# Latent projections ahead of the context's feed-forward network, which runs beside the window attention, with the modulations one stage earlier

## The chip, the cores and the metric

The kernel runs on one core of a Trainium2 chip. A core has a matrix engine (TensorE, PE, whose weight loads are listed as PEld), a vector engine (VectorE, DVE), a scalar engine (ScalarE, ACT), a general engine (GpSimd, POOL) and a queue engine (SyncE, SP), which here issues every transfer between the device's main memory and the on-chip buffers. The metric is the device time of one execution in microseconds (us); lower is better.

## The reference, cut to what matters

A token stream x (512 tokens of 1024) passes two hybrid layers; then it and a context stream xc (256 tokens) pass two more blocks. The change concerns the first of those, the even block:

```python
for l in range(DEPTH):
    sh1, sc1, g1, sh2, sc2, g2 = split(s_c @ ada_w[l] + ada_b[l], 6)      # and csh1 ... cg2 from s_cc
    h  = rms_norm_2(x,  norm_g[l, 0]) * (1 + sc1)  + sh1
    hc = rms_norm_2(xc, norm_g[l, 0]) * (1 + csc1) + csh1
    y, yc = mixer_even(h, hc, ...)
    x = x + g1 * rms_norm_2(y, norm_g[l, 1])
    h = rms_norm_2(x, norm_g[l, 2]) * (1 + sc2) + sh2
    x = x + g2 * rms_norm_2(swiglu(h, ffn_w_in[l], ffn_w_out[l]), norm_g[l, 3])
    if l < DEPTH - 1:                                                      # the context, even block only
        xc = xc + cg1 * rms_norm_2(yc, norm_g[l, 1])
        hc = rms_norm_2(xc, norm_g[l, 2]) * (1 + csc2) + csh2
        xc = xc + cg2 * rms_norm_2(swiglu(hc, ffn_w_in[l], ffn_w_out[l]), norm_g[l, 3])

def mixer_even(h, hc):
    qa, ka, va, cq, ckv, kpe = split_cols(h @ w_in, EVEN_SIZES)            # window q, k, v; latents of q and kv; rotary key
    qb  = rms_norm_2(cq,  q_norm)  @ w_uq                                  # 8 heads of 64 + 32 rotary
    kvb = rms_norm_2(ckv, kv_norm) @ w_ukv                                 # 8 heads of 64 key + 64 value
    oa = windowed_sink_attention(qa, ka, va, ka_c, va_c, sink)             # local window and the context
    ob = softmax attention of qb over the keys of context and tokens
    return concatenate([oa, ob]) @ w_out
```

## The kernel before

**Products.** Activations lie with channels on the partitions, 8 tiles of 128 (KD = 8) by the tokens. Every product in single precision is taken as three products of halves: `split` makes hi and lo of an activation, `weights` loads 128 x 1024 of a weight (512 KB, tile wr, three buffers), lets ACT cast it to wh and POOL, or for every third one DVE, form wl (two buffers each). `dense` then does 24 matmuls for 128 output channels: wh with hi and lo for each of 8 input tiles, and wl with hi. `fm(i)` in `even_project` is such a dense with columns of ev_w_in: 0 to 3 window queries, 4 window key, 5 window value, 6 the latent of keys and values, 7 and 8 that of queries, 9 the rotary key.

**Memory.** The operand h of the token stream lies in hh and hl (2 x 16 KB a partition). Smaller tiles come from pool rp (nine buffers). Results that attention needs in another layout go by `put` (line 816) to scratch in main memory and come back by `get` (line 819): eka and eva (window key, value), eqm (window queries), ekn, ekp, evb (latent attention's key, rotary key, value), eqnm and eqpm (its queries). An rp tile is free again once its write has landed. All puts, gets and loads go through SP in one order.

**Order.** Each engine runs its instructions in the order of the program. `weave` runs several streams (Python generators) by turns in proportion to their rates; a third number is an offset in priority. `background` holds the modulations (`mods`: a chunk loads 2 tiles mr of ada_w, makes products with the two condition vectors and spreads them), and `tick` moves them on by a rate while a weave runs; `drain` finishes them. Twelve chunks of the groups (4, 3, 5) concern this block's second half.

**Stages around the change**, all in the function that quotes `even_project` (lines 1810 to 1860): `ctxa`, the second layer's output projection beside the context's own attention; `ctxo`, the residual and norm that give h (`boundary`) beside the context's output projection; `evp`, first `win()` (window projections fm 0 to 5) beside the context's residual, then in `win` the window attention `even_window` (two groups of four query heads, four blocks each) beside `lat()`. That `lat()` is in order: fm 6 and its norm; four products with ev_w_ukv for the keys, whose eight tiles are put to ekn; four products for the values (evb); fm 9 and the rotary key; fm 7, 8 and their norm; the products with ev_w_uq (eqnm, eqpm). After that come `lat`, the latent attention `even_latent` beside `context()` (norm, feed-forward network of the context (FFN), second norm, in memory of pool cf), the output projection, and the boundary before the main FFN, beside what is left of `context()`. In that weave the context has rate 48 to the attention's 9.6, and it stops when the attention ends.

## Time and profile before

| | us |
|---|---|
| three runs | 2822.88, 2830.22, 2830.51 |
| their median | 2830.22 |
| profiled execution | 2819.89 |
| its span in the trace | 2818.1 |
| PE busy | 2455.0 (87%) |
| DVE, ACT, POOL busy | 1258.7, 1188.2, 1079.4 |
| mean granted clock of PE | 0.918 |

The profile comes from one more execution. Stages are cut at instructions found in the trace: the first matmul with ev_w_in, the first window score, the first latent score, the first and last matmul of the output projection, and the first matmul of the main FFN.

### The profile page before, as it was taken

Reading aid. Unit: us, or ns where it says so; the run is one execution under the profiler, and the core shown is the slowest. Engines: PE = TensorE matmul, PEld = TensorE weight load, DVE = VectorE, ACT = ScalarE, POOL = GpSimd, SP = SyncE. Lnnn points to the kernel's source line nnn. Section 1 sums busy time; section 2 is a strip of 40 time slices with the busy share of each in tenths; the row PEclk is TensorE's granted clock in tenths of the full one; section 3 lists DMA queues with packets and bytes.
Section 4 is the critical chain, followed back from the end, with each engine's and each line's share of the span. In section 5 each row is a group of like instructions: output and inputs, shape, how many; then the busy total and the mean of one; then the engine's idle time right before and its main releaser. Section 6 shows DMA issues by size and latency. Waiting matters only on the chain. (4 is left out here: it accounts for less than half of the span.)

```text
span 2818.1 us, 35394 instructions
## 1 busy us (share of the span) xinstructions
PE 2455.0 (87%) x13052; PEld 1994.9 (71%) x13052; DVE 1258.7 (45%) x2065; ACT 1188.2 (42%) x2227; POOL 1079.4 (38%) x754
## 2 busy tenths in 40 slices
PE   6988896778888886769999899999888989799997
PEld 4765666666666665648998777777776777688886
DVE  3655357235646644445442631212645767421212
ACT  3534365333547534445554522222434646332222
POOL 2435235344533551213455732322542222443334
PEclk9988998888979987879999999999988989899998
DMA  7364644344344652335553545454444253333332
GB/s 244 121 205 156 207 165 154 107 140 162 104 124 139 213 182 100 116 112 143 174 159 135 186 135 172 149 169 133 148 140 158 90 153 113 113 100 97 94 97 75
DMA packets 170816, 400.56 MB, mean 142 GB/s; under 512 B 19378, under 2 KB 60820, under 8 KB 167316
## 3 DMA queue, kind: packets, MB, share of 16 engines
q1 hardware_dynamic: 170644, 398.31, 43.7%
q8 instruction: 103, 1.69, 0.2%
q14 instruction: 69, 0.57, 0.1%
HBM read 339.85 MB, written 58.39 MB: 141 GB/s over the span
## 5 line engine op out<-in xcount | busy, mean ns | idle before, releaser
L398 POOL TENSOR_TENSOR wl<-wr,wh 128x1024 fp32r<-128x1024 f32 (+3 forms) x245 | 538.2, 2198 | 899.5 <-ACT wh L422 451.5
L422 ACT CAST wh<-wr 128x1024 fp32r<-128x1024 f32 (+3 forms) x367 | 353.8, 964 | 706.5 <-PE d L389 279.5
L389 PE MATMUL d<-hh,wh 128*128 128x512 f32 x960 | 398.4, 415 | 19.7 <-ACT hh L556 7.8
L389 PE MATMUL d<-hl,wh 128*128 128x512 f32 x960 | 394.0, 410 | 1.9 <-DVE hl L557 0.9
L389 PE MATMUL d<-hh,wl 128*128 128x512 f32 x960 | 263.5, 403 | 0.0
L400 DVE SCALAR_TENSOR_TENSOR wl<-wr,wh 128x1024 fp32r<-128x1024 f32 (+3 forms) x122 | 152.1, 1246 | 227.8 <-PE d L389 91.9
L389 PEld LDWEIGHTS d<-hh,wh 128*128 128x128 f32 x960 | 190.6, 199 | 62.2 <-ACT hh L556 8.4
L389 PEld LDWEIGHTS d<-hl,wh 128*128 128x128 f32 x960 | 189.7, 198 | 42.5 <-issue 2.5
L389 PEld LDWEIGHTS d<-hh,wl 128*128 128x128 f32 x960 | 185.0, 195 | 39.6 <-issue 1.6
L400 DVE SCALAR_TENSOR_TENSOR pg<-b,pg 128x512 fp32r<-128x512 f32 (+1 forms) x208 | 137.2, 665 | 68.7 <-ACT pg L404 67.2
L389 PE MATMUL b<-hh,wh 128*128 128x512 f32 x416 | 164.2, 395 | 0.0
L389 PE MATMUL b<-hl,wh 128*128 128x512 f32 x416 | 163.2, 392 | 0.0
L934 POOL TENSOR_TENSOR oy<-pg,pg 64x256 f32<-64x256 f32 (+1 forms) x72 | 57.7, 802 | 262.3 <-DVE pg L932 91.3
L404 ACT CAST pg<-b 128x512 fp32r<-128x512 f32 (+1 forms) x208 | 117.1, 570 | 80.2 <-PE b L909 68.2
L882 DVE TENSOR_REDUCE sm<-s 128x1 f32<-128x768 f32 (+3 forms) x144 | 120.7, 846 | 26.6 <-PE s L389 25.9
L389 PE MATMUL d<-hc,wh 128*128 128x256 f32 x656 | 105.4, 311 | 23.7 <-DVE rp L400 11.8
L950 DVE SCALAR_TENSOR_TENSOR rp<-rp,d 128x512 f32<-128x512 f32 (+1 forms) x77 | 46.7, 607 | 165.5 <-ACT rp L949 165.4
L1745 DVE SCALAR_TENSOR_TENSOR rp<-rp,b 128x512 f32<-128x512 f32 (+1 forms) x64 | 38.1, 595 | 175.3 <-PE b L389 174.8
L389 PE MATMUL d<-hid,wh 128*128 128x512 f32 (+1 forms) x528 | 114.7, 361 | 1.5 <-POOL hid L398 1.5
L389 PEld LDWEIGHTS d<-hc,wh 128*128 128x128 f32 x656 | 94.9, 211 | 28.3 <-ACT wh L422 12.2
L389 PE MATMUL b<-hid,wh 128*128 128x512 f32 (+1 forms) x528 | 110.8, 361 | 0.0
L389 PE MATMUL b<-hh,wl 128*128 128x512 f32 x416 | 103.8, 389 | 0.0
(416 smaller groups left out, 5143.2 us busy)
## 6 DMA issues: line engine op xcount, KB each, us to landing
wr<-in_ffn_w_in SPq DMA_DIRECT2D x132, 512.0 KB
mr<-in_ada_w SPq DMA_DIRECT2D x96, 512.0 KB
wr<-in_ffn_w_out SPq DMA_DIRECT2D x48, 512.0 KB
x<-x SPq DMA_DIRECT2D x20, 1024.0 KB
wr<-in_w_in SPq DMA_DIRECT2D x38, 512.0 KB
mr<-in_w_mod SPq DMA_DIRECT2D x32, 512.0 KB
wr<-in_ev_w_in SPq DMA_DIRECT2D x20, 512.0 KB
wr<-in_ffn_w_out SPq DMA_DIRECT2D x24, 384.0 KB
```

Source lines behind the costliest of these rows:

```text
L389: self.nc.tensor.matmul(out, lhsT, rhs, start=start, stop=stop)
L398: self.nc.gpsimd.tensor_sub(out, src, hi)
L400: self.nc.vector.scalar_tensor_tensor(out, src, scale, hi, op0=ALU.mult, op1=ALU.subtract)
L404: self.nc.scalar.copy(hi, src)
L422: nc.scalar.copy(hi[:, :n], raw[:, :n])
L882: nc.vector.reduce_max(c, s, axis=AX.X, negate=True)
L934: nc.gpsimd.tensor_tensor(d, sel(t), sel(rs), op=ALU.mult)
L950: nc.vector.scalar_tensor_tensor(t, t, 1.0, ps, op0=ALU.add, op1=ALU.mult)
L1745: nc.vector.scalar_tensor_tensor(g, g, 0.5, pu, op0=ALU.mult, op1=ALU.mult)
```

## The change

- `even_project` is rearranged for the token stream: after fm 6 come fm 7 and 8 (`queries()`, tiles latq) and fm 9 (`rotary_key()`), and only then ukv and uq. The context's own order stays.
- The first three steps of `lat()` now run ahead of the window attention (`first(lt, 3)`), so that h is read for the last time before it.
- `context()` starts beside the window attention, with rate 22 to 8 (attention) and 4 (`lat`). Its operand lies in the memory of hl, its hidden units in that of hh. Pool cf goes. In the latent stage its rate is 36 instead of 48.
- The output projection reads its operand from a new pool `oh` (two tiles of 16 KB) in place of hh and hl.
- Modulations (4, 3, 5) run at rate 0.55 instead of 0.3 and are drained before `evp` rather than behind the window stage.
- The window attention has four query buffers instead of five.

```diff
--- before.py
+++ after.py
@@ -537,12 +537,12 @@
             except StopIteration as e:
                 return e.value
 
-    def prenorm_steps(self, x, T, gain, shift, pool=None, al=None):
+    def prenorm_steps(self, x, T, gain, shift, pool=None, al=None, into=None):
 
         nc = self.nc
         n = x.shape[1]
         r = self.rstd(self.square_sums([x[:, k, :] for k in range(n)], T, al), T, al=al)
-        h = self.new_h(T, pool)
+        h = into or self.new_h(T, pool)
         for k in range(n):
             self.norm_tile(h, x, k, T, r, gain, shift, al)
             yield
@@ -1417,7 +1417,7 @@
             self.split_ps(src, d[:, :, 0, :], d[:, :, 1, :])
             self.put(self.eva[:, c0 // 128 + t], d.rearrange("p h a d -> p h (a d)"))
 
-    def latent(self, fs, T, gains, pool):
+    def latent(self, fs, T, gains, pool, name="lat"):
 
         nc = self.nc
         xs = []
@@ -1429,7 +1429,7 @@
         out = []
         for i, (x, g) in enumerate(zip(xs, gains)):
             nc.vector.scalar_tensor_tensor(x, x, g, r, op0=ALU.mult, op1=ALU.mult)
-            hl = [self.tl(pool, [128, T], F32R, f"lat{i}{p}", 1) for p in range(2)]
+            hl = [self.tl(pool, [128, T], F32R, f"{name}{i}{p}", 1) for p in range(2)]
             self.split(x, *hl)
             out.append(hl)
         return out
@@ -1453,28 +1453,11 @@
             self.vtrans(fm(5), T, c0)
             yield
 
-        def latent():
-
-            (ck,) = self.latent([partial(fm, 6)], T, [self.mla_gain[:, 2:3]], pool)
-            hi, lo = self.weights(I["ev_w_ukv"], 1024)
-            for i in range(4):
-                w = slice(i * 128, i * 128 + 128)
-                ps = self.three(self.bank([128, T], "d"), [(hi[:, w], lo[:, w])], [ck])
-                parts = self.rp([128, T], F32R), self.rp([128, T])
-                self.split_ps(ps, *parts)
-                for hl, p in enumerate(parts):
-                    self.put(self.ekn[hl, :, 2 * i:2 * i + 2, c0:c0 + T].rearrange("r h t -> h r t"), p)
-            yield
-            for t in range(T // 128):
-                tok = slice(t * 128, t * 128 + 128)
-                ps = self.bank([128, 512], "d")
-                self.mms(ps, [(ck[0][:, tok], hi[:, 512:]), (ck[1][:, tok], hi[:, 512:]), (ck[0][:, tok], lo[:, 512:])])
-                for g in range(2):
-                    v = self.rp([128, 4, 2, 64], F32R)
-                    src = ps[:, g * 256:g * 256 + 256].rearrange("p (h d) -> p h d", d=64)
-                    self.split_ps(src, v[:, :, 0, :], v[:, :, 1, :])
-                    self.put(self.evb[:, c0 // 128 + t, 4 * g:4 * g + 4, :], v.rearrange("p h a d -> p h (a d)"))
-            yield
+        def queries():
+            gains = [self.mla_gain[:, 0:1], self.mla_gain[:, 1:2]]
+            return self.latent([partial(fm, 7), partial(fm, 8)], T, gains, pool, "latq" if rope else "lat")
+
+        def rotary_key():
 
             ps = fm(9)
             hi, lo = self.rp([32, T], F32R), self.rp([32, T])
@@ -1490,11 +1473,42 @@
                 self.split_ps(ps[0:32], hi, lo)
             for hl, p in enumerate((hi, lo)):
                 self.put(self.ekp[hl, :, c0:c0 + T], p)
-            yield
-
-            cq = self.latent([partial(fm, 7), partial(fm, 8)], T, [self.mla_gain[:, 0:1], self.mla_gain[:, 1:2]], pool)
+            return tab
+
+        def latent():
+
+            (ck,) = self.latent([partial(fm, 6)], T, [self.mla_gain[:, 2:3]], pool)
+            if rope:
+                yield
+                cq = queries()
+                yield
+                tab = rotary_key()
+                yield
+            hi, lo = self.weights(I["ev_w_ukv"], 1024)
+            for i in range(4):
+                w = slice(i * 128, i * 128 + 128)
+                ps = self.three(self.bank([128, T], "d"), [(hi[:, w], lo[:, w])], [ck])
+                parts = self.rp([128, T], F32R), self.rp([128, T])
+                self.split_ps(ps, *parts)
+                for hl, p in enumerate(parts):
+                    self.put(self.ekn[hl, :, 2 * i:2 * i + 2, c0:c0 + T].rearrange("r h t -> h r t"), p)
+            yield
+            for t in range(T // 128):
+                tok = slice(t * 128, t * 128 + 128)
+                ps = self.bank([128, 512], "d")
+                self.mms(ps, [(ck[0][:, tok], hi[:, 512:]), (ck[1][:, tok], hi[:, 512:]), (ck[0][:, tok], lo[:, 512:])])
+                for g in range(2):
+                    v = self.rp([128, 4, 2, 64], F32R)
+                    src = ps[:, g * 256:g * 256 + 256].rearrange("p (h d) -> p h d", d=64)
+                    self.split_ps(src, v[:, :, 0, :], v[:, :, 1, :])
+                    self.put(self.evb[:, c0 // 128 + t, 4 * g:4 * g + 4, :], v.rearrange("p h a d -> p h (a d)"))
+            yield
+            if not rope:
+                tab = rotary_key()
+                yield
+                cq = queries()
+                yield
             sb = 96 ** -0.5
-            yield
 
             def up(hi, lo, i):
                 w = [slice(i * 256 + k * 128, i * 256 + k * 128 + 128) for k in range(2)]
@@ -1811,7 +1825,7 @@
             nc.sync.dma_start(xc, I["ctx"])
             mp = self.phase("mp")
             self.mp = mp.__enter__()
-            self.background(self.mods(ada[0], I["ada_w"][0], (4, 3, 5)), 0.3)
+            self.background(self.mods(ada[0], I["ada_w"][0], (4, 3, 5)), 0.55)
             with self.phase("ctxa") as ph:
                 at = self.area(ph, "c", kp=1, k=4, q=8, v=3, p=8)
                 y, sq = self.weave((self.out_proj(I["w_out"][1], mix[0], S, *mix[1:]), 8, 30),
@@ -1826,32 +1840,39 @@
                 self.close_y()
             yc, sqc = done["result"]
             self.stage(low=3, split=100, turn=100)
+            self.drain()
+            mp.__exit__(None, None, None)
+            half = lambda tag: self.tl(self.sb, [128, 2, KD, CL], F32R, tag, 1)
+
+            def context():
+                hc = half("hl")
+                yield from self.prenorm_steps(xc, CL, *mc(2), into=(hc[:, 0], hc[:, 1]))
+
+                def hid():
+                    t = half("hh")
+                    return t[:, 0], t[:, 1]
+
+                yf, sqf = yield from self.ffn(0, (hc[:, 0], hc[:, 1]), CL, hid)
+                yield from self.postnorm_steps(xc, yf, sqf, CL, mc(3))
+
+            rest = context()
             with self.phase("evp") as ph:
                 sc, win, lat = self.even_project(h, S, CL, True, ph)
                 self.weave((win(), 4.8, 0), (self.postnorm_steps(xc, yc, sqc, CL, mc(1)), 12.0, 0))
                 o = self.oy(S)
                 with self.phase("win") as ph:
-                    at = self.area(ph, "e", k=2, q=5, v=1, p=8)
-                    self.weave((self.even_window(at, sc["q"], o[0]), 8, 0), (lat(), 7, -50))
-            self.drain()
-            mp.__exit__(None, None, None)
+                    at = self.area(ph, "e", k=2, q=4, v=1, p=8)
+                    lt = lat()
+                    self.weave((self.chain(self.first(lt, 3), self.woven((self.even_window(at, sc["q"], o[0]), 8, 0),
+                                                                         (lt, 4, 0), (rest, 22, -100), until=True)), 20, 0))
+                    self.steps(lt)
             self.stage(low=3, turn=30)
-            with self.phase("cf") as cf:
-                def context():
-                    hc = yield from self.prenorm_steps(xc, CL, *mc(2), pool=cf)
-
-                    def hid():
-                        t = self.tl(cf, [128, 2, KD, CL], F32R, "hid", 1)
-                        return t[:, 0], t[:, 1]
-
-                    yc, sqc = yield from self.ffn(0, hc, CL, hid)
-                    yield from self.postnorm_steps(xc, yc, sqc, CL, mc(3))
-
-                rest = context()
+            with self.phase("oh") as oh:
+                ho = [oh.tile([128, KD, S], F32R, name=self.name("oh")) for _ in range(2)]
                 with self.phase("lat") as ph:
                     at = self.area(ph, "e", kp=1, k=2, q=2, v=1, p=4)
-                    self.weave((self.even_latent(at, sc, S, TK, o[1]), 9.6, 0), (rest, 48, 100), until=True)
-                y, sq = self.result(self.out_proj(I["ev_w_out"], self.split_o(o, S, self.new_h(S)), S))
+                    self.weave((self.even_latent(at, sc, S, TK, o[1]), 9.6, 0), (rest, 36, 100), until=True)
+                y, sq = self.result(self.out_proj(I["ev_w_out"], self.split_o(o, S, ho), S))
                 h = self.weave((self.boundary(y, sq, x2, m(1), m(2), x3), 18, 60), (rest, 14.4, 0))
             g2 = m(3)
             self.stage(low=3)
```

Where instructions now stand. In the rows the number behind a name tells one buffer of that name from the next.

The SP queue in `ctxo`, from the row behind the last store of x up to the first weights of ev_w_in (mr are loads of ada_w), before:

```order
L750 DMA mr_8656<-in_ada_w 128x1024
L417 DMA wr_8763<-in_ev_w_out 128x1024
L750 DMA mr_8714<-in_ada_w 128x1024
L417 DMA wr_8809<-in_ev_w_out 128x1024
L750 DMA mr_8803<-in_ada_w 128x1024
L417 DMA wr_8871<-in_ev_w_out 128x1024
L750 DMA mr_8865<-in_ada_w 128x1024
L417 DMA wr_8931<-in_ev_w_in 128x1024
L417 DMA wr_9019<-in_ev_w_in 128x1024
```

and after the change, there:

```order
L750 DMA mr_8672<-in_ada_w 128x1024
L750 DMA mr_8693<-in_ada_w 128x1024
L417 DMA wr_8863<-in_ev_w_out 128x1024
L750 DMA mr_8733<-in_ada_w 128x1024
L750 DMA mr_8757<-in_ada_w 128x1024
L417 DMA wr_8927<-in_ev_w_out 128x1024
L750 DMA mr_8796<-in_ada_w 128x1024
L750 DMA mr_8862<-in_ada_w 128x1024
L417 DMA wr_8973<-in_ev_w_out 128x1024
L750 DMA mr_8899<-in_ada_w 128x1024
L750 DMA mr_8926<-in_ada_w 128x1024
L417 DMA wr_9054<-in_ev_w_in 128x1024
```

Ahead of the first ev_w_in weight stand eight loads of ada_w behind that store, and stood four.

ACT in the window stage, at the last of the latent key's splits (rp from d), with the exponentials (ep) of the window attention behind them, before:

```order
L404 CAST rp_9558<-d_9554 128x512
L887 ACTIVATE ep_9739,sm_9730<-s_9731,sm_9729 128x512
L925 COPY pg_9667<-d_9611 64x512
L931 COPY pg_9669<-b_9670 64x512
L404 CAST pg_9782<-b_9777 128x512
L404 CAST rp_9685<-d_9681 128x4x64
L887 ACTIVATE ep_9749,sm_9730<-s_9741,sm_9729 128x512
L404 CAST pg_9793<-b_9788 128x512
L404 CAST rp_9689<-d_9681 128x4x64
```

and after:

```order
L404 CAST rp_9770<-d_9766 128x512
L503 ACTIVATE rp_9779<-xc 128x256
L503 ACTIVATE rp_9781<-xc 128x256
L503 ACTIVATE rp_9783<-xc 128x256
L503 ACTIVATE rp_9786<-xc 128x256
L503 ACTIVATE rp_9789<-xc 128x256
L503 ACTIVATE rp_9792<-xc 128x256
L503 ACTIVATE rp_9795<-xc 128x256
L503 ACTIVATE rp_9798<-xc 128x256
L404 CAST pg_9880<-b_9875 128x512
L887 ACTIVATE ep_9837,sm_9828<-s_9829,sm_9827 128x640
```

The eight squares of the context's norm (line 503, from xc) come in behind the key's splits and ahead of the next exponentials; the splits of the value (rp_9685 and on before) come later.

PE at the first scores (s from ek and eq) of the second head group; pg and ev are the window attention's weights and values. Before, a dense of the token stream (d_9850, from hh and hl) is woven in:

```order
L389 MATMUL d_9776<-pg_9827,ev_9309 128x512
L389 MATMUL s_9909<-ek_9891,eq_9897 128x256
L389 MATMUL s_9919<-ek_9891,eq_9899 128x256
L389 MATMUL d_9850<-hl_8753,wh_9846 128x512
L389 MATMUL d_9850<-hh_8752,wh_9846 128x512
L389 MATMUL d_9850<-hl_8753,wh_9846 128x512
L389 MATMUL d_9850<-hh_8752,wh_9846 128x512
L389 MATMUL d_9850<-hl_8753,wh_9846 128x512
L909 MATMUL b_9966<-ident,ep_9739 128x128
```

and after, the first dense of the context's FFN (from hl, 256 columns):

```order
L389 MATMUL s_10227<-ek_10202,eq_10207 128x256
L389 MATMUL s_10227<-bmask_r,ident_r 128x256
L389 MATMUL s_10227<-ek_10199,eq_10207 128x256
L389 MATMUL s_10227<-ek_10202,eq_10207 128x256
L389 MATMUL d_10137<-hl_9776,wh_10133 128x256 x12
L389 MATMUL b_10168<-hl_9776,wh_10164 128x256
L909 MATMUL b_10263<-ident,ep_9966 128x128
L909 MATMUL b_10263<-ident,ep_9976 128x128
L909 MATMUL b_10263<-ident,ep_9986 128x128
L909 MATMUL b_10263<-ident,ep_9996 128x128
L389 MATMUL b_10168<-hl_9776,wh_10164 128x256 x8
L389 MATMUL s_10237<-ek_10199,eq_10209 128x256
```

The denses with hh and hl are gone from the stage, and the FFN's first stands here.

PE from the last eight matmuls of the output projection on. Before, the context's FFN (hc) follows:

```order
L389 MATMUL b_13705<-hh_13435,wl_13702 128x512 x8
L389 MATMUL s_13812<-blk,rp_13487 128x1 x3
L389 MATMUL d_13750<-hc_10905,wh_13746 128x256
L389 MATMUL s_13812<-blk,rp_13487 128x1
L389 MATMUL d_13750<-hc_10905,wh_13746 128x256 x10
L389 MATMUL s_13812<-blk,rp_13731 128x1 x4
L389 MATMUL d_13750<-hc_10905,wh_13746 128x256 x4
L498 MATMUL s_13825<-ident,sm_13823 128x128 x4
L389 MATMUL d_13750<-hc_10905,wh_13746 128x256
L389 MATMUL d_13750<-hc_10905,wl_13747 128x256 x8
L389 MATMUL b_13781<-hc_10905,wh_13777 128x256 x16
L389 MATMUL b_13781<-hc_10905,wl_13778 128x256 x8
```

and after, two denses of its end (hh, 256 columns), then sums of squares (blk) and their transposes (sm):

```order
L389 MATMUL b_14287<-oh_11481,wl_14284 128x512 x8
L389 MATMUL d_14331<-hh_13088,wh_14327 128x256 x11
L389 MATMUL s_14354<-blk,rp_14313 128x1 x4
L389 MATMUL d_14331<-hh_13088,wh_14327 128x256
L389 MATMUL d_14331<-hh_13088,wl_14328 128x256 x3
L498 MATMUL s_14367<-ident,sm_14365 128x128 x4
L389 MATMUL d_14331<-hh_13088,wl_14328 128x256 x3
L389 MATMUL b_14381<-hh_13088,wh_14377 128x256 x12
L389 MATMUL b_14381<-hh_13088,wl_14378 128x256 x6
L389 MATMUL b_14408<-blk,rp_13793 128x1 x2
L389 MATMUL b_14408<-blk,rp_14401 128x1 x2
L498 MATMUL b_14417<-ident,sm_14415 128x128 x2
```

Of the context's FFN 54 matmuls stand in the output projection and the boundary, and stood 422.

## Rows read from the trace of the kernel before

**Rows 1.** The page: span; PE's busy time; the cast of weights on ACT

```profile
span 2818.1 us, 35394 instructions
...
PE 2455.0 (87%) x13052; PEld 1994.9 (71%) x13052; DVE 1258.7 (45%) x2065; ACT 1188.2 (42%) x2227; POOL 1079.4 (38%) x754
...
L422 ACT CAST wh<-wr 128x1024 fp32r<-128x1024 f32 (+3 forms) x367 | 353.8, 964 | 706.5 <-PE d L389 279.5
```

**Rows 2.** Windows by stage: stretch, length, busy per engine, clock, DMA share, GB/s

```profile
953.00:1000.80 47.80, 38.03 (x292) 33.08 (x292) 34.01 (x51) 28.22 (x56) 32.44 (x26) 0.82 0.67 240
1000.80:1048.10 47.30, 41.76 (x197) 32.03 (x195) 15.32 (x28) 9.02 (x15) 21.67 (x15) 0.89 0.49 164
1048.10:1147.84 99.74, 55.36 (x267) 43.34 (x267) 38.97 (x91) 36.79 (x85) 12.22 (x11) 0.74 0.38 131
1147.84:1249.65 101.81, 75.95 (x418) 60.33 (x418) 51.92 (x106) 47.92 (x101) 27.06 (x22) 0.84 0.33 104
1249.65:1285.00 35.35, 27.94 (x116) 22.16 (x117) 18.91 (x31) 18.03 (x38) 4.15 (x5) 0.74 0.34 89
1285.00:1493.30 208.30, 204.37 (x1556) 192.14 (x1555) 105.91 (x144) 118.27 (x196) 95.49 (x50) 1.00 0.57 169
1493.30:1536.70 43.40, 43.40 (x193) 35.90 (x192) 4.47 (x5) 17.15 (x23) 19.60 (x11) 1.00 0.33 112
1536.70:1604.60 67.90, 58.70 (x455) 56.26 (x453) 49.30 (x61) 36.56 (x60) 50.35 (x31) 0.95 0.48 153
```

**Rows 3.** Waits of PE, 1036 to 1280: for what, total us, times, longest

```profile
PE b L389 <- ACT pg L931: 16.3, 2, 16.0
PE d L389 <- DVE rp L400: 11.2, 3, 7.4
PE s L389 <- DMA evb<-rp: 9.1, 1, 9.1
...
PE d L389 <- DMA ev<-eva: 5.6, 1, 5.6
```

**Rows 4.** Timeline of SP's queue, 1040 to 1250: start, length, transfer, count

```profile
1097.44 30.49 SPq L816 DMA_DIRECT2D ekn<-rp  x8
...
1190.36 30.42 SPq L816 DMA_DIRECT2D eqnm<-rp  x8
```

**Rows 5.** Window over the ekn writes, columns as in rows 2

```profile
1097.00:1130.00 33.00, 16.97 (x87) 12.47 (x85) 13.61 (x31) 12.53 (x31) 1.46 (x2) 0.74 0.13 48
```

**Rows 6.** Waits of ACT, 1048 to 1250

```profile
ACT rp L404 <- DMA ekn<-rp: 22.5, 6, 4.8
...
ACT rp L503 <- DMA eqnm<-rp: 13.9, 3, 4.8
ACT wh L422 <- DMA wr<-in_ev_w_in: 13.7, 1, 13.7
```

**Rows 7.** Timelines of PE: one modulation chunk's products; one dense of 256 columns

```profile
995.87 1.07 PE L389 MATMUL b<-mr,mc 128*32 128x256 f32 x16
996.87 0.61 PE L389 MATMUL b<-mod_sel,ms 128*128 128x2 f32 x4
...
1542.71 2.05 PE L389 MATMUL b<-hc,wh 128*128 128x256 f32 x16
1544.60 1.10 PE L389 MATMUL b<-hc,wl 128*128 128x256 f32 x8
1545.54 2.05 PE L389 MATMUL d<-hc,wh 128*128 128x256 f32 x16
```

**Rows 8.** Timeline of SP's queue, 970 to 1001, behind the store of x

```profile
974.33 0.37 SPq L750 DMA_DIRECT2D mr<-in_ada_w  x1
...
988.73 5.14 SPq L417 DMA_DIRECT2D wr<-in_ev_w_in  x2
```

**Rows 9.** Timeline of PE at a later boundary without context work

```profile
2411.27 1.07 PE L389 MATMUL b<-hh,wl 128*128 128x512 f32 x4
...
2436.16 0.79 PE L389 MATMUL d<-hh,u0h 128*128 128x512 f32 x1 [1.60 <-ACT hh L556]
```

More of the change, by code (lines that the diff above doesn't have):

```diff
@@ L1454, in window @@
             yield
+        def queries():
+            gains = [self.mla_gain[:, 0:1], self.mla_gain[:, 1:2]]
+            return self.latent([partial(fm, 7), partial(fm, 8)], T, gains, pool, "latq" if rope else "lat")
+        def rotary_key():
+            ps = fm(9)
+            hi, lo = self.rp([32, T], F32R), self.rp([32, T])
+            tab = self.load_tab(I["rope3"], T, pool) if rope else None
+            if rope:
+                b, sk = self.rp([32, T]), self.rp([64, T])
+                nc.sync.dma_start(sk, I["sin3k"])
+                nc.vector.tensor_tensor(lo, ps[0:32], tab[0][0:32], op=ALU.mult)
+                nc.vector.tensor_tensor(b, ps[32:64], sk[32:64], op=ALU.mult)
+                nc.vector.tensor_add(lo, lo, b)
+                self.split(lo, hi, lo)
+            else:
+                self.split_ps(ps[0:32], hi, lo)
+            for hl, p in enumerate((hi, lo)):
+                self.put(self.ekp[hl, :, c0:c0 + T], p)
+            return tab
         def latent():
             (ck,) = self.latent([partial(fm, 6)], T, [self.mla_gain[:, 2:3]], pool)
+            if rope:
+                yield
[3 more added lines that the diff above has]
+                yield
             hi, lo = self.weights(I["ev_w_ukv"], 1024)
@@ L1477, in latent @@
             yield
-            ps = fm(9)
-            hi, lo = self.rp([32, T], F32R), self.rp([32, T])
-            tab = self.load_tab(I["rope3"], T, pool) if rope else None
-            if rope:
-                b, sk = self.rp([32, T]), self.rp([64, T])
-                nc.sync.dma_start(sk, I["sin3k"])
-                nc.vector.tensor_tensor(lo, ps[0:32], tab[0][0:32], op=ALU.mult)
-                nc.vector.tensor_tensor(b, ps[32:64], sk[32:64], op=ALU.mult)
-                nc.vector.tensor_add(lo, lo, b)
-                self.split(lo, hi, lo)
-            else:
-                self.split_ps(ps[0:32], hi, lo)
-            for hl, p in enumerate((hi, lo)):
-                self.put(self.ekp[hl, :, c0:c0 + T], p)
-            yield
-            cq = self.latent([partial(fm, 7), partial(fm, 8)], T, [self.mla_gain[:, 0:1], self.mla_gain[:, 1:2]], pool)
+            if not rope:
[3 more added lines that the diff above has]
+                yield
             sb = 96 ** -0.5
-            yield
             def up(hi, lo, i):
```

## The prediction

> **What bounds the kernel now.** I read the page's head first: of a span of 2818.1 us TensorE (PE) is busy 2455.0, 87% [rows 1]. The chain of waits at the end of the page covers only the last stage, so it says nothing about the place of the change; I cut the span into the stages that the diff touches and read busy time and granted clock of each [rows 2]. [...]
>
> - context output projection (953.0 to 1000.8): work 38.03 x 0.82 = 31.2, loses 16.6
> - A, window projections (to 1048.1): 41.76 x 0.89 = 37.2, loses 10.1
> - B, window attention beside the latent projections, in two head groups: 55.36 x 0.74 = 41.0 of 99.74 and 75.95 x 0.84 = 63.8 of 101.81. Together it loses 97 of 201.6 us, by far the most
> - C, latent attention beside the context's FFN: the first 35.35 us lose 14.7, the next 208.3 are full (204.37 at clock 1.00)
> - output projection: full (43.40 of 43.4); boundary: 58.70 x 0.95 = 55.8 of 67.9, most of it context FFN
>
> So C has no room, B has much, and the change carries PE work from C and the boundary to B. What B waits for stands in the waits of PE [rows 3]: a 16.0 us wait for an attention copy at B's end, 11.2 us for rp tiles, 9.1 for a window operand behind the latent writes, 5.6 for a value tile. I read the second and third as effects of the SP queue: two trains of eight writes to ekn and eqnm hold it 30.5 us each [rows 4], and while the first runs the 16 DMA engines are busy 13% [rows 5]. Splits that need an rp tile wait 22.5 us on ACT for the first train, 13.9 for the second [rows 6].
>
> **Prices.** One 512-column matmul: 43.40 us / 192 = 0.226, so 5.4 us for a dense of 24 [rows 2]. One dense of 256 columns: 1545.54 - 1542.71 = 2.83 us, 0.118 a matmul [rows 7]. One chunk of modulations: from 995.87 to 997.48, 1.6, say 1.7 us, and 1 MB to load [rows 7].
>
> **Part 1, modulations one stage up.** Six of the twelve chunks leave A (2) and B (4) for the two context stages, which already do the other six. PE: 6 x 1.7 = 10.2 us. SP: behind the store of x, eight ada_w loads instead of four stand ahead of the first ev_w_in weight; now 3.5 MB are issued between 974.33 and 988.73 [rows 8], and 2 MB more at the stage's 240 GB/s [rows 2] are 8.7 us. Lower bound +3 (the 16.6 us that the stage loses take most), upper +18 (PE and DMA one after the other). The drain is paced by loads, so I lean on the DMA figure plus a little PE: **+11**.
>
> **Part 2, A.** Four denses more (queries' two, latent key, rotary key): 96 x 0.226 = +21.7; two chunks fewer, -3.4. More weights in a row through three buffers: between 0 and the 13.7 us that ACT once waited for such a weight [rows 6]; A's DMA share of 0.49 [rows 2] puts it near the low end, I take 4. **+22** (range +18 to +32). The weights' splits go along on ACT and POOL, busy 9.02 and 21.67 of 47.3 us in A.
>
> **Part 3, B.** Out: four denses (21.7) and four chunks (6.8). In: 384 + 144 FFN matmuls, 528 x 0.118 = 62.3. Work 104.8 - 28.5 + 62.3 = 138.6. The FFN's splits, 22 on ACT at 0.964 [rows 1] = 21 us, are hidden beside ACT's 84.7 busy us in B's 201.6; without that cover they would stand in PE's way one by one, which is the second rival.
> Group 1 gets no FFN matmuls: in the new order the first stands behind group 2's first scores. It loses one dense and two chunks at clock 0.74, (5.4 + 3.4) / 0.74 = 11.9, the 5.6 us wait for the value tile, and part of the rp waits, since the rotary key's tiles are out of the way: 99.7 less 12, 6 and 4, **78**. The ekn train stays. Eight squares for the context's norm, each wanting an rp tile, now stand on ACT right behind the last ekn splits and ahead of the next block's exponentials; before, it was evb splits that stood in turn between exponentials. Between 0 and another 22.5 us (the existing wait for that train [rows 6]); I take 0, because the same number of tiles was already wanted there.
> Group 2: work 63.8 - 16.3 - 3.4 + 62.3 = 106.4. Stalls: 16.0 + 9.1 and the losses at half clock made 38 (101.81 - 63.8). The FFN covers the 16.0 us wait, as it does in C, where PE is full. The eqnm train stays, but four FFN weights are ahead of it or within it; a train of 30 us holds what comes after, and four denses are 11.3 us. I take 14 us of loss, between 2% of the work (C's second part) and the present 38: **120**.
> B is then 198, **-3**. Lowest 162 (below), highest 245 (below).
>
> **Part 4, C.** 1002 instead of 1152 FFN matmuls: -150 x 0.118 = -17.7. The start loses 14.7 now; with weights loaded and hidden units ready I take 5 (bounds 0 and 14.7, nearer the full part). **-28**, bounds -12 (C held by its own softmax chain) and -33.
>
> **Part 5, output projection and boundary.** They hold 422 matmuls of FFN and its tail now, 54 after. Output projection 43.4 + 18 x 0.118 = 45.5. A boundary without such filling is in the trace once more: last output matmul from 2411.27 on, first dense at 2436.16 [rows 9], 24 us. To this come up to 36 x 0.118 = 4.2 of FFN left, and the context's last norm on the same DVE and ACT; the first dense then goes at the pace of the norm's tiles. I take 33 (24 to 42): 79 instead of 111.3, **-32** (-25 to -40). What is lost here is cover: FFN that ran for nothing in the boundary's waits has to find other waits, in B.
>
> **Sum.** 11 + 22 - 3 - 28 - 32 = **-30**. The separate 32 KB pool costs nothing: it is written as hh/hl were, and the main FFN waits for hh/hl only until the last context matmul, which stands in the boundary. The profiled execution took 2819.89 (span 2818.1); it is the shortest of four (2819.89, 2822.88, 2830.22, 2830.51; their mean 2825.9, the median of the three runs 2830.22). I put the change on the mean: **2796 us** (2790 for an execution like the profiled one).
>
> [...] The trace shows the train slow while the DMA engines are 87% idle [rows 4, 5], so a write of two rows of 64 x 512 seems to go over few engines. [...]
>
> **Rivals.**
> *More is gained (0.17).* The train's wait on ACT and SP is fully covered and group 1 shrinks too: B = work 138.6 + losses of 23 (a quarter of now) = 162, 36 less: **2760**. For it: C shows FFN matmuls filling an attention to 98%. Against: group 1 has none.
> *Slower (0.15).* FFN weights are now issued just ahead of and behind the writes, on one queue, and PE takes its instructions in order: an FFN dense whose weight is late holds the scores, products and projections behind it. If nothing of the 97 us is filled, B = 138.6 + 97 = 235, and if two denses stand for a third of a train besides, 245: 47 more than forecast, **2843**. It decides from B above 228, losses above 90. For it: ten FFN loads stand ahead of the two trains or within them. Against: three weight buffers run ahead.
> *Given back (0.18).* The drain is paced by its own chain of load, product and broadcast (+21 instead of +11), and C is held by its own softmax chain once it has less filling (-12 instead of -28): 26 more, **2822**, within what can be told from none.
> That the work does not move is excluded by the new order: 528 FFN matmuls stand in B.
>
> **Chances.** Forecast 0.50, the rivals 0.17, 0.15, 0.18. Range: from a little below the first rival, **2752**, over the third to **2828**; only the second lies outside. About 0.3% (8.5 us) is what a measurement of this kernel can tell from no change. Faster by more: 0.47 of the forecast + 0.17 + 0.06 of the third = 0.70; within: 0.03 + 0.12 = 0.15; slower: 0.15.
>
> **What would show it.** Windows of the new trace, cut at the same instructions: context stages 11 longer; A about 69; group 1 about 78 and group 2 about 120, with clock above 0.9 in group 2; C about 215 with PE full to the end; output projection and boundary about 79. Wrong, if PE in B waits on weight splits (wh or wl) for tens of us (second rival), if the ekn wait on ACT grows through the squares, or if the eight loads stretch the context stage by 20.

## The result, and the profile after

The changed kernel took 2853.94 us (median of four runs, 2850.44 to 2858.47), the kernel before 2828.24 beside it: ratio 1.0103, 95% interval 1.008 to 1.0126 (the quotient of the two medians, 1.009, lies in it). It is slower by 1%. Forecast were 2796 us and a range of 2752 to 2828.

The profiled execution has a span of 2848.7 us, 30.6 more than before, so the two traces carry the whole difference. The stages of the changed kernel, cut at the same instructions, are in order: context output projection (from 953.00 on in both, so it holds what the modulations delayed just before), A, B in its two head groups (the second from its first score product, in both kernels the 65th with ek in the stage), C, output projection, boundary (columns as in [rows 2]):

```profile
953.00:1025.79 72.79, 57.25 (x406) 47.55 (x407) 36.22 (x63) 33.97 (x69) 34.03 (x27) 0.79 0.64 231
1025.79:1108.61 82.82, 66.35 (x293) 53.74 (x293) 27.20 (x47) 21.62 (x34) 32.77 (x22) 0.88 0.47 149
1108.61:1181.34 72.73, 39.56 (x202) 32.40 (x201) 38.16 (x86) 32.77 (x81) 11.41 (x12) 0.74 0.19 64
1181.34:1344.85 163.51, 118.42 (x804) 107.12 (x802) 81.69 (x122) 72.50 (x136) 57.72 (x37) 0.89 0.38 119
1344.85:1563.29 218.44, 209.55 (x1514) 193.38 (x1514) 113.87 (x159) 121.69 (x207) 83.97 (x46) 0.98 0.53 158
1563.29:1612.27 48.98, 48.31 (x220) 39.49 (x221) 5.07 (x6) 19.70 (x28) 25.81 (x16) 1.00 0.38 137
1612.27:1639.03 26.76, 11.43 (x70) 10.16 (x69) 19.02 (x31) 9.55 (x17) 15.84 (x12) 0.67 0.50 174
```

Work, here as in the prediction, is TensorE's busy time times its granted clock, and what a stage loses is its length less that. The product is right to some 6%: in the changed kernel 512-column matmuls follow each other by 0.426 us at a granted clock of 0.50 (1089.59 to 1091.72) and by 0.227 us at 1.00 (1094.33 to 1097.73). The half clock of the prediction's part 3 is 0.50 too (1220 to 1225 of the kernel before).

Against [rows 2], in us:

| stage | before | after | change | forecast |
|---|---|---|---|---|
| context output projection | 47.8 | 72.8 | +25.0 | +11 |
| A, window projections | 47.3 | 82.8 | +35.5 | +22 |
| B, window attention | 201.6 | 236.2 | +34.7 | -3 |
| C, latent attention | 243.7 | 218.4 | -25.2 | -28 |
| output projection and boundary | 111.3 | 75.7 | -35.6 | -32 |
| sum up to the main FFN | | | +34.4 | -30 |

What was to be gained came, 61 us in the last two rows. What was to cost 30 us in the first three cost 95, and 38 of the missing 65 are in B. (The stretch behind the main FFN's first matmul is 3.8 us shorter, hence 30.6 in the span.) B has two holes. TensorE's longest waits between 1025 and 1346 (what for, total, times, longest) and the timeline rows at which the two longest end:

```profile
PE s L389 <- ACT ep L887: 26.1, 1, 26.1
PE b L389 <- DVE rp L518: 22.6, 1, 22.6
PE b L389 <- ACT rp L503: 11.8, 1, 11.8
PE b L909 <- ACT ep L887: 5.7, 2, 4.0
PE s L389 <- DMA eq<-eqnm: 5.2, 1, 5.2
```

```profile
1156.24 1.01 PE L389 MATMUL b<-blk,rp 128*128 128x1 f32 x4 [22.64 <-DVE rp L518]
...
1272.60 1.01 PE L389 MATMUL s<-ek,eq 128*128 128x384 f32 x2 [26.08 <-ACT ep L887]
```

Neither named engine is the cause; one goes back along what that engine itself waited for. ACT's timeline at both places:

```profile
1144.66 0.42 ACT L503 ACTIVATE rp<-xc 128x256 f32<-128x256 f32 x1 [4.77 <-DMA ekn<-rp]
1149.72 1.03 ACT L503 ACTIVATE rp<-xc 128x256 f32<-128x256 f32 x3 [4.65 <-DMA ekn<-rp]
1154.85 0.42 ACT L503 ACTIVATE rp<-xc 128x256 f32<-128x256 f32 x1 [4.10 <-DMA ekn<-rp]
...
1241.21 1.04 ACT L422 CAST wh<-wr 128x1024 fp32r<-128x1024 f32 x1 [7.42 <-DMA wr<-in_ffn_w_in]
...
1268.08 1.04 ACT L422 CAST wh<-wr 128x1024 fp32r<-128x1024 f32 x1 [25.52 <-DMA wr<-in_ffn_w_in]
```

The first hole is the squares of the context's norm: behind the first two, ACT waits four times, 4 to 5 us each, until a write of the ekn train has landed and freed an rp tile (three of the waits are shown). On TensorE the sum of these squares stands ahead of the window attention, so that waits too. The second is an FFN weight. SP's queue there:

```profile
1126.45 30.48 SPq L816 DMA_DIRECT2D ekn<-rp  x8
...
1221.70 5.54 SPq L816 DMA_DIRECT2D eqnm<-rp  x3
1227.87 3.60 SPq L417 DMA_DIRECT2D wr<-in_ffn_w_in  x1
1231.56 21.90 SPq L816 DMA_DIRECT2D eqnm<-rp  x5
1253.55 28.28 SPq L417 DMA_DIRECT2D wr<-in_ffn_w_in  x6
```

One weight stands within the eqnm train, the next behind it: issued at 1253.55 and not cast before 1268.08. ACT takes its instructions in order, the window's exponentials are behind that cast, and the scores behind the exponentials: 26 us of TensorE for a context weight. The DMA view of 1215 to 1275, in 40 slices of 1.5 us (busy tenths of the 16 engines, then GB/s), shows the train as a plateau at about 51 GB/s, with a share of 0.13 (1240 to 1252), as much as 2 of the 16 engines all the time (0.125):

```profile
DMA  0360011111166111111111111111159951110046
GB/s 0 71 279 0 0 22 27 49 52 52 60 145 265 51 51 52 55 49 52 49 52 52 51 51 52 52 51 51 52 128 401 382 210 52 55 49 38 0 106 243
```

### The profile page after: what moved, and what is told of

It reads as the page before. It is cut to its first block, busy times and chain, and to the rows that moved or that the text cites. A ratio compares the mean times of both kernels' runs of the same rounds, so it can differ in the third digit from the quotient of the medians.

```text
span 2848.7 us, 35416 instructions
## 1 busy us (share of the span) xinstructions
PE 2460.6 (86%) x13052; PEld 2003.3 (70%) x13052; DVE 1264.5 (44%) x2065; ACT 1190.5 (42%) x2227; POOL 1073.1 (38%) x754
## 5 line engine op out<-in xcount | busy, mean ns | idle before, releaser
L389 PE MATMUL d<-hl,wh 128*128 128x512 f32 (+1 forms) x1280 | 435.3, 379 | 3.9 <-POOL hl L398 1.4
L389 PE MATMUL d<-hh,wh 128*128 128x512 f32 (+1 forms) x1104 | 416.5, 397 | 21.7 <-ACT hh L556 9.5
L389 PE MATMUL d<-hh,wl 128*128 128x512 f32 (+1 forms) x1016 | 270.9, 395 | 0.0
L389 PEld LDWEIGHTS d<-hl,wh 128*128 128x128 f32 x1280 | 231.8, 197 | 46.3 <-POOL hl L398 3.4
L400 DVE SCALAR_TENSOR_TENSOR wl<-wr,wh 128x1024 fp32r<-128x1024 f32 (+3 forms) x122 | 149.5, 1225 | 213.9 <-PE d L389 93.7
L389 PE MATMUL b<-hl,wh 128*128 128x512 f32 (+1 forms) x736 | 203.8, 344 | 3.0 <-ACT wh L422 3.0
L389 PE MATMUL b<-hh,wh 128*128 128x512 f32 (+1 forms) x560 | 176.5, 362 | 0.0
L400 DVE SCALAR_TENSOR_TENSOR pg<-b,pg 128x512 fp32r<-128x512 f32 (+1 forms) x208 | 137.0, 666 | 67.9 <-ACT pg L404 66.8
L882 DVE TENSOR_REDUCE sm<-s 128x1 f32<-128x768 f32 (+3 forms) x144 | 121.3, 848 | 31.4 <-PE s L389 30.6
L389 PEld LDWEIGHTS b<-hl,wh 128*128 128x128 f32 x736 | 120.7, 193 | 18.7 <-ACT wh L422 3.3
L389 PE MATMUL b<-hh,wl 128*128 128x512 f32 (+1 forms) x472 | 108.5, 369 | 0.0
L389 PEld LDWEIGHTS b<-hh,wh 128*128 128x128 f32 x560 | 96.2, 192 | 16.0 <-ACT wh L422 0.2
L483 POOL TENSOR_TENSOR sm<-sm,mhalf 128x4 f32<-128x4 f32 (+3 forms) x33 | 46.3, 1404 | 148.8 <-DVE sm L481 138.6
```

The source lines that it names most:

```text
L389: self.nc.tensor.matmul(out, lhsT, rhs, start=start, stop=stop)
L400: self.nc.vector.scalar_tensor_tensor(out, src, scale, hi, op0=ALU.mult, op1=ALU.subtract)
L483: nc.gpsimd.tensor_tensor(r, ms, self.mhalf[:, None, :].to_broadcast([128, nt, n]), op=ALU.pow)
L882: nc.vector.reduce_max(c, s, axis=AX.X, negate=True)
```

## Experiments

Theory W: the trains of writes to ekn and eqnm make both holes, as they made much of B's loss before, and the changed kernel only puts more behind them. Rivals: the place of the squares; the modulations; the order of the latent projections. Ratios below are to the kernel before, run beside each.

| kernel | us | ratio, 95% interval |
|---|---|---|
| changed kernel | 2853.94 | 1.0103 (1.008 to 1.0126) |
| after_spread | 2782.85 | 0.9858 (0.9835 to 0.988) |
| before_spread | 2748.83 | 0.9742 (0.9709 to 0.9775) |
| before_split_time | 2828.95 | 1.0009 (0.9988 to 1.003) |
| after_sq_first | 2860.01 | 1.013 (1.0105 to 1.0156) |
| after_mods_late | 2837.13 | 1.0051 (1.0033 to 1.007) |
| mods_up_alone | 2836.97 | 1.0054 (1.0035 to 1.0072) |
| latents_first_alone | 2807.99 | 0.9953 (0.993 to 0.9976) |
| before_spread_all | 2768.12 | 0.9823 (0.9796 to 0.9851) |
| after_three_mended | 2754.56 | 0.9764 (0.974 to 0.9787) |
| spread_latents_first | 2739.73 | 0.9702 (0.9672 to 0.9731) |
| spread_latents_q | 2739.77 | 0.9702 (0.9677 to 0.9726) |

**The trains: after_spread and before_spread.** Each write of two heads becomes two of one head, the same for eqnm:

```diff
-                    self.put(self.ekn[hl, :, 2 * i:2 * i + 2, c0:c0 + T].rearrange("r h t -> h r t"), p)
+                    for j in range(2):
+                        self.put(self.ekn[hl, :, 2 * i + j, c0:c0 + T], p[64 * j:64 * j + 64])
```

> The changed kernel, with each write of two 64-row heads to ekn and eqnm issued as two writes of 64 rows (16 instead of 8 per train). Theory W: the two long waits of TensorE in the window stage (22.6 us for the sum of squares behind the ekn train, 26.1 us for a score behind a weight held by the eqnm train) come from those trains, 30.5 us each, because such a write keeps 2 of 16 DMA engines and SP's queue. Then both waits nearly vanish, the trains take under 10 us each, the window stage falls from 236 to about 190 us and the time from 2854 to about 2810, below the kernel before (2828). Rival: the stage is held by the nine rp tiles or by the weights' splits, whatever the writes take; then the time stays above 2845.

> The kernel before, with the same split of the writes. Theory W: the waits of 11.2 us (rp tiles) and 9.1 us (a window operand) go, and part of the 16.0 us at the stage's end: 15 to 30 us, 2800 to 2813. Rival: the stage before is bound by the attention's own chain of scores, maxima and exponentials, and those waits only change their name: 2823 to 2830.

In after_spread B, up to the first rotary score, is 192 us instead of 238, and the two holes are gone; the longest waits of TensorE from 1082 to 1275 are

```profile
PE s L389 <- DMA eq<-eqnm: 6.7, 1, 6.7
PE b L909 <- ACT ep L887: 5.7, 2, 4.0
PE b L389 <- DVE rp L518: 4.7, 1, 4.7
```

The expected size was too low (71 us for 44): the context's own writes to ekn and eqnc, in earlier stages, have the same form and are split by the same edit, and the context output projection ends 23 us earlier too (1002.7). The surprise is before_spread: 72 us, not 15 to 30. Its B is 155 us instead of 203 (both up to the first rotary score, 1.4 us later than in [rows 2]), and the rest came earlier. Its trains on SP, and the DMA view of 1075 to 1090:

```profile
1077.01 10.60 SPq L816 DMA_DIRECT2D ekn<-rp  x16
1136.69 14.15 SPq L816 DMA_DIRECT2D eqnm<-rp  x16
```

```profile
DMA  0000000068989898898998979891498898999998
GB/s 0 0 0 0 0 0 0 0 147 186 224 186 218 208 202 202 180 229 202 202 213 186 268 169 197 202 191 44 137 213 208 186 224 191 202 224 186 344 377 333
```

SP is through with the same bytes after 10.6 us instead of 30.5 [rows 4], at some 200 GB/s. So theory W holds, though its price for the kernel before was less than half of what was measured, and the changed kernel is behind the kernel before with either form of write: by 1.0% with the old one, by 1.2% (0.9858 against 0.9742) with the new. The holes are thus not what made it slower than the kernel before: they took in the changed kernel what the same trains, in other waits, took before.

**A control: before_split_time.** Also twice as many writes, but cut along the tokens:

```diff
-                    self.put(self.ekn[hl, :, 2 * i:2 * i + 2, c0:c0 + T].rearrange("r h t -> h r t"), p)
+                    for j in range(2):
+                        u = slice(j * T // 2, (j + 1) * T // 2)
+                        self.put(self.ekn[hl, :, 2 * i:2 * i + 2, c0 + j * T // 2:c0 + (j + 1) * T // 2].rearrange("r h t -> h r t"), p[:, u])
```

> A control for before_spread: the kernel before, with each write to ekn and eqnm also issued as two, but cut along the tokens (2 x 64 x 256) instead of by head (64 x 512). If what made the trains short is the number of engines, set by the slowest dimension, each train still takes about 30 us, and the time is 2815 to 2840. Rival: if smaller writes, or twice as many of them, are what helps, the trains take 10 to 15 us and the time is near 2749.

```profile
1109.11 37.86 SPq L816 DMA_DIRECT2D ekn<-rp  x16
1203.45 37.82 SPq L816 DMA_DIRECT2D eqnm<-rp  x16
```

The DMA view of its ekn train, 1110 to 1145:

```profile
DMA  0111112111111111111111111111111111111111
GB/s 20 34 34 48 48 48 68 48 48 48 48 49 48 48 48 49 48 48 48 48 49 48 48 49 48 48 48 48 49 48 48 49 47 49 48 48 49 48 48 48
```

The trains are longer than the 30 us expected, and nothing is gained. The writes are as many and as large as in before_spread, but between one and two tenths of the 16 engines are busy, not eight or nine tenths. So neither the number nor the size of the writes decides, but the two heads as slowest dimension. (The rows are also half as long here, 1 KB; whether that makes the train longer is open.) In the kernel before the ekn train shows a DMA share of 0.13 and 51 GB/s (1115 to 1130), and behind the writes of 4 x 32 rows to eqm, four heads as slowest dimension, it is 0.26 and 102 GB/s (1040 to 1042; behind the next four of them 0.26 to 0.27 and 100 to 104, 1060 to 1064); that these bytes are theirs is inferred from the order of SP's queue. Two and four of 16 engines would be 0.125 and 0.25. Which engines a write goes over, no view shows.

**The squares: after_sq_first.**

```diff
-                    self.weave((self.chain(self.first(lt, 3), self.woven((self.even_window(at, sc["q"], o[0]), 8, 0),
+                    self.weave((self.chain(self.first(lt, 3), self.first(rest, 1), self.woven((self.even_window(at, sc["q"], o[0]), 8, 0),
```

> The changed kernel, with the first step of the context's norm (its eight squares and the sum) ahead of the latent key's products, so that they no longer stand behind the ekn train on ACT. If the 22.6 us wait is the place of the squares behind that train, it goes and the time falls by about 20 to 2834, while the 26.1 us wait behind the eqnm train stays. If the train holds whatever wants an rp tile next (the splits of the value, the exponentials behind them), another wait of 15 us or more takes its place and the time stays above 2846.

B is 243.2 us instead of 237.7 by the same cut, the time no better. The 22.6 us wait is 6.8 now; others took its place. Longest waits of TensorE in that B, and what DVE waits for at its start (1112 to 1190):

```profile
PE s L389 <- ACT ep L887: 25.2, 6, 21.1
PE d L389 <- ACT pg L404: 15.5, 4, 11.2
PE b L909 <- DVE pg L400: 10.9, 4, 5.1
PE b L389 <- ACT wh L422: 8.1, 1, 8.1
PE b L389 <- DVE rp L518: 6.8, 1, 6.8
```

```profile
DVE rp L554 <- DMA ekn<-rp: 16.8, 5, 4.7
```

The tiles of the norm itself, which follow the squares, now want the rp tiles that the train holds, on DVE, and the window attention's maxima stand behind them. So the place of the squares was only where the train showed.

**The three parts: after_mods_late, mods_up_alone, latents_first_alone.** The first is the changed kernel with the modulations as before, the second the kernel before with only them moved, the third the kernel before with only the new order of `lat()`. For memory the window attention has seven buffers for its weights in the first and the third, and four for queries in the third.

> The changed kernel, with the modulations as before (rate 0.3, drained behind the window stage; the window attention gets seven instead of eight buffers for its weights, for memory). If the 25 us by which the context output projection grew are the six chunks moved there, it ends 25 us earlier; six chunks (10 us of TensorE) return to the stages with idle time, so the time is 2829 to 2838. If the chunks' loads then stand behind the write trains and hold TensorE there, most is given back and the time stays above 2845.

> The kernel before, with only the modulations one stage up (rate 0.55, drained ahead of the window projections). In the changed kernel the late modulations ended the context output projection 21.8 us earlier, and cost 6 us more in the window stage. If the move by itself is a loss of that size, the time rises by 10 to 18 us over the kernel before; the stage up to the first window dense ends 22 to 25 us later, and A and B give 5 to 12 back. Rival: the 16 us wait at the window stage's end, whose waiting matmul is a modulation's product, belongs to the chunks; then B gives back 16 or more and the time is within 5 us of the kernel before.

> The kernel before, with only the latent projections ahead of the window attention (queries and rotary key ahead of ukv; four query buffers, seven for the weights); the context's FFN and the modulations stay. The changed kernel's stage A grew by 35 us, 11.8 of it one wait for squares that want rp tiles, for 21.7 us of matmuls. If A's growth is of the order alone, A is 78 to 83 here too, and the window stage falls by less than A grows, because its losses behind the write trains stay: the time is 8 to 20 us above the kernel before. Rival: the window stage falls by as much (203 to 170), and the order is neutral; then the long waits of the changed kernel are the FFN's alone.

The modulations cost 0.54% alone, and 0.52% (1.0103 less 1.0051) within the change: 15 us both ways. Alone, they end the context output projection 21 us later (1021.9) and give 3 us back in B; the rival, 16 us back, falls.

The order of the latents is a gain: 0.47%, which I had put as a loss. A does grow, to 80 us, but the window stage falls from 203 to 156. A and window stage of latents_first_alone:

```profile
995.39:1075.44 80.05, 70.33 (x349) 54.34 (x348) 25.59 (x48) 23.03 (x38) 34.08 (x23) 0.94 0.60 200
1075.44:1231.68 156.24, 96.78 (x536) 76.35 (x535) 80.19 (x177) 71.26 (x162) 27.00 (x26) 0.83 0.30 99
```

Work in the stage falls by 24 us (104.8 to 96.78 x 0.83 = 80.3) and its losses by 22 (98 to 76), although both trains stay.

What is left of the change is the FFN in the window stage, with its memory and its rates: after_mods_late less latents_first_alone, 1.0051 less 0.9953, is **+0.98%, 28 us**. By parts: 0.54 - 0.47 + 0.98 = 1.05%, and 1.03% was measured for the whole; each part is uncertain by some 0.2 to 0.3%.

**The same on mended writes: after_three_mended and spread_latents_first.** The first is the changed kernel with split writes, squares first and late modulations; the second latents_first_alone with split writes.

> The changed kernel with split writes to ekn and eqnm, the squares ahead of the latent key's products, and the modulations late (seven buffers for the attention's weights). With split writes alone it took 2783. Late modulations give 15 to 20, and the FFN can start in the first head group, where TensorE was busy 41 of 58 us: 0 to 15 more. So 2750 to 2768. If the window stage's losses can be filled by the FFN once weights come in time, it gets below the 2749 of the kernel before with split writes; if the FFN only moves its time from one stage to another, it does not.

> The kernel before, with the latent projections ahead of the window attention (as in latents_first_alone, which gained 12 us) and the writes to ekn and eqnm split (which gained 72 us alone). FFN and modulations stay as before. If the two gains are of different waits, they add: 2730 to 2742, below all kernels so far; the FFN in the window stage is then a loss of 12 to 25 us even where its weights come in time, since after_three_mended, which has both and the FFN there besides, took 2754.6. Rival: the order gained only because its products ran clear of the trains; then the time is 2745 to 2755 and the FFN costs nothing there.

Window stage, C, output projection and boundary, of spread_latents_first and then of after_three_mended:

```profile
1066.58:1176.65 110.07, 89.91 (x536) 70.49 (x535) 80.62 (x177) 70.59 (x161) 27.18 (x25) 0.95 0.50 141
1176.65:1414.78 238.13, 225.52 (x1668) 208.22 (x1668) 124.81 (x175) 135.98 (x233) 99.69 (x54) 0.99 0.56 161
1414.78:1458.49 43.71, 43.71 (x197) 36.20 (x195) 4.61 (x5) 17.27 (x23) 19.63 (x12) 1.00 0.35 111
1458.49:1526.79 68.30, 60.07 (x453) 57.93 (x454) 49.00 (x61) 36.58 (x60) 50.81 (x31) 0.93 0.47 155
```

```profile
1068.57:1251.26 182.69, 157.39 (x1096) 137.55 (x1094) 113.32 (x218) 106.77 (x220) 70.36 (x49) 0.97 0.49 143
1251.26:1466.70 215.44, 206.85 (x1524) 191.58 (x1523) 113.55 (x160) 122.65 (x209) 86.60 (x50) 1.00 0.56 164
1466.70:1519.78 53.08, 49.73 (x204) 39.42 (x203) 5.69 (x5) 18.37 (x26) 24.38 (x15) 0.94 0.32 113
1519.78:1546.00 26.22, 8.94 (x54) 7.51 (x52) 18.53 (x33) 8.10 (x15) 15.04 (x11) 0.60 0.43 160
```

This is the answer on the change itself. With short trains, and with the latents first, the window stage is 110 us with 89.91 x 0.95 = 85 of work: 25 us are free, not 97. The FFN there adds 72.6 us for 552 of its matmuls, 65 us by [rows 7]; nothing of it is hidden. Out of C and the boundary it takes 22.7 and 42.1 us, and the output projection grows by 9.4. Together +17 us, 0.62% (0.9764 less 0.9702). No run put fewer FFN products there or gave them another rate; whether 25 us of them would run for nothing is open. spread_latents_first, with spread_latents_q at the same time, is the fastest kernel of the study: 3.0% below the kernel before and 4% below the changed one.

**Other writes: before_spread_all and spread_latents_q.** All writes of several heads split, and then only the token stream's window queries (4 x 32 rows) beside ekn and eqnm.

> The kernel before, with all writes of several heads issued head by head, also those of 4 x 32, 2 x 32 and 8 x 16 rows (window queries and keys, hybrid layers, odd block). With ekn and eqnm alone so split it took 2749. If a write goes over as many engines as its slowest dimension lets, a write of 4 x 32 over 4 should gain too, though less: 2725 to 2743. Rival: these were not waited for, and the larger number of issues on SP costs as much: 2745 to 2760.

> As spread_latents_first, with the token stream's window queries (writes of 4 x 32 rows to eqm) also issued head by head. before_spread_all had a window stage of 139 us instead of 155, and lost 23 us earlier, at the hybrid layers and the context. If those 16 us were the window queries' writes, 8 to 16 us below spread_latents_first; if the issues on SP, four for one, eat it, within 5 us of it or above.

Split everywhere, the window stage gains 16 us more (139 against 155), but the stretch ahead of it loses 23 and A 6: 2768. With the latents first, splitting the window queries gives nothing (window stage 108.5 against 110.1). For those writes nothing is won. That the additional issues on SP eat it (for the context's window queries, eqc, 32 of a median 0.42 us, against 8 of 0.57 in before_spread) is a guess, and which of the earlier writes costs the 23 us stays open.

## Why the prediction was wrong

**Part 3, B, is the step that failed, in the loss of group 2.** B took 236 us for 198: group 2 took 163.5 for 120, group 1 72.7 for 78. Group 2's work came as forecast, 118.42 x 0.89 = 105 us for 106. Its loss I put at 14 us because C is full; it was 58, more than the 38 of before, and 26.1 of it is the one weight behind the eqnm train. In after_spread, with short trains, the same group is 135.71 us long and loses 135.71 - 116.06 x 0.97 = 23. The second rival described that (weights on one queue with the trains, TensorE in order, B at 245): B measured 236 and the time 2854 for its 2843. I gave it 0.15 with three buffers as counter-argument; they do not help when SP itself is held for 22 us. The sign I had named for it, tens of us of TensorE waiting on weight splits, did not show (3.0 us in B): the late weight held ACT, and TensorE waited for the exponentials behind it.

In group 1 a wait of 22.6 us for the squares came where I had added 0. Yet the group lost 72.73 - 39.56 x 0.74 = 43 us, where my 78 us held 46 and the kernel before lost 58.7. The squares wait for the same train as the splits that stood in their place, with exponentials behind those too, and ACT waits 18.1 us for it where it had waited 22.5 [rows 6]. As an addition to the loss of before the 0 was right.

**Behind it is a misreading of B's 97 us.** I read idle TensorE as room. The runs show that 48 us of B came and went with the trains (203 to 155), and 22 us of its losses with the order. With the trains, the stage's other streams waited for the same queue and tiles that the FFN needs as well, so the FFN could not run there; that the 22 us of the order were of this kind too is not shown. Only 25 us of B were room, and the FFN needs 62. The boundary that it left was better room: there it had filled a wait, and the boundary lost only 67.9 - 55.8 = 12 us with it [rows 2], and 26.76 - 11.43 x 0.67 = 19 without.

**Part 1 was mis-sized**: +25.0 (+21 alone) for +11, above its bound of +18. The stage's work grew by 57.25 x 0.79 - 31.2 = 14 us and its losses by 11, so the upper bound's case, matmuls and loads one after the other, is nearer than mine. On SP the chunks' loads come in pairs, each paced by the products of the chunk before (between 953 and 1030 the loads of ada_w wait 23.3 us for TensorE):

```profile
989.12 0.81 SPq L750 DMA_DIRECT2D mr<-in_ada_w  x2
...
995.05 0.80 SPq L750 DMA_DIRECT2D mr<-in_ada_w  x2
...
1004.75 0.80 SPq L750 DMA_DIRECT2D mr<-in_ada_w  x2
```

and TensorE waits 8.3 us for a chunk's sums on DVE. The mechanism was that of the third rival, whose +21 is nearer.

**Part 2 was mis-sized**: +35.5 for +22. The work grew by 66.35 x 0.88 - 37.2 = 21 us, where 21.7 - 3.4 = 18 were counted: the denses bring 32 small matmuls along (the latents' sums of squares and transposes). The loss grew by 14, where I took 4 for the weights. 11.8 of it is one wait for a latent's squares; ACT came late to them because it had stood 8.4 us before an rp tile that a window query's write held:

```profile
1082.00 0.27 ACT L404 CAST rp<-b 128x128 fp32r<-128x128 f32 x1 [8.42 <-DMA eqm<-rp]
...
1085.03 1.86 PE L389 MATMUL b<-blk,rp 128*128 128x1 f32 x8 [11.79 <-ACT rp L503]
```

The norms' need of rp tiles was not in the sum. latents_first_alone has A at 80 us without this wait (its squares wait 0.5), but its A holds three chunks of modulations, which the changed kernel has moved away, so the two lengths do not compare.

**Part 4 and part 5 were right**: -25.2 for -28, -35.6 for -32. TensorE is busy in 209.55 of C's 218.44 us, and the bare boundary of [rows 9] was the right row: 26.76 us with some FFN in it. In part 5 two errors of opposite sign met, by luck: the output projection took 49.0 us for 45.5, the boundary 26.8 for 33.

**On the write that seemed to go over few engines** I left the sum by rows as it was, and a weight late behind a train to the second rival. Few engines for two heads is seen: a share of 0.13 and 51 GB/s for the form with two heads, eight or nine tenths and 200 GB/s for one. A weight that waits behind a train has a row now: 14.5 us from issue to use (1253.55 to 1268.08), and in B ACT waits 32.9 us for such weights, in after_spread at most 2.2. On which engines the weight waited no row shows.

## What to carry to other kernels

Idle time of an engine is room only for work that does not need what the stage waits for: ask which queue or buffer holds the stage, and whether the work to be moved there needs it too. Here the cheapest test was to shorten the suspected holder in the kernel before; it was worth 2.6% and, with the latents first, 3.0%, and with both 25 us of room were left, not 97. When a load may come late, ask who stands behind the instruction that waits for it, on each engine that runs in order: here the cast of a context weight held the window's exponentials, and these the scores.

## What the runs showed of the hardware

A write of 256 KB whose slowest dimension is two heads moved at about 51 GB/s and in the two trains before held SP's queue for 3.8 us each on average (30.49 / 8, [rows 4]); as two writes of one head the same bytes went at about 200 GB/s, and cut along the tokens they stayed slow (48 GB/s, 37.9 us a train). That a change at two places in how a scratch tile is written would be worth 72 us, beside a kernel whose TensorE is busy 87%, I had not expected: I had priced the trains at their two named waits of 20 us.
